# Norm factors folded into output weights, the residual factor folded into norm constants, and pauses in the background weight splitting of a two-layer decoder kernel

## The chip, the core and the metric

The kernel runs on one core of one Trainium2 chip. A core has a matrix engine (TensorE, PE in the profile, with its weight load shown apart as PEld), a vector engine (VectorE, DVE), a scalar engine (ScalarE, ACT), a general engine (GpSimd, POOL), and a queue processor (SyncE, SP) that here issues all transfers between the chip's memory (HBM) and the on-chip buffers (SBUF; matmul results land in PSUM). Each engine works through its own instructions in order and waits on semaphores for the others. The metric is the device time of one execution in microseconds.

## What is computed

Two layers of a decoder trunk over 1024 tokens with 1024 features, in float32. Layer 0 is gated linear attention, layer 1 an indexed sparse attention. The change touches layer 0 only. Cut to what matters:

```python
def gla_mixer(x, ...):                  # layer 0, four heads, 512 value features each
    ...                                 # q, k, v, z, gate from x @ w_in; chunked recurrence gives o
    o = o * rsqrt(mean(o * o, -1) + 1e-5)          # per token and head
    o = o.reshape(B, L, 2048) * gn_g               # one factor per feature
    return (o * silu(z)) @ w_out

for i in range(2):
    y = mixer_i(x)
    x = layer_norm(ALPHA * x + y, ln_g[i], ln_b[i])     # ALPHA = 4 ** 0.25, eps 1e-5
    x = x + (p[i] @ ple_w[i]) * sigmoid(x @ ple_gate_w[i])
```

## The kernel before

**Matmuls in two parts.** Every float32 operand of a large matmul is split in a rounded high part and a low part (high = copy rounded by ACT, low = difference by DVE), and each product is three matmuls: high x high, high x low, low x high. `split` (L387) does so for activations: ACT first, DVE 0.9 us of planned time later.

**Order by a planner.** The program is written out by Python code that keeps a planned time `fl.now`, which grows with each matmul that is issued (`Flow`, L48). Work can be put on a heap with a due time (`at`, `after`, `chain`), and between groups of three matmuls `pace` (L108) issues what is due and then calls the pacers: the weights, and three background generators `bg`, `bg2`, `bg3`. All this decides only the order of instructions on each engine; on the chip the engines keep to that order and wait for semaphores.

**Weights.** `Weights` (L138) loads the 128x1024 weight tiles in the order of `seq` into `wst` (two buffers, L189), and splits each in four steps of 512 columns: two ACT copies into `whi` (L173), two DVE subtractions into `wlo` (L175), one step each 1.15 us of planned time, two to three tiles ahead of their use.

**Splitting ahead.** `split_ahead` (L193) runs in `bg3` during layer 0. Layer 1's weights, used by both halves of the tokens, are split once and the parts stored in HBM. It works in pieces of 512 columns: load `pst` (L200, two buffers), ACT copy `phi` (L209), store `whs` (L211) and load of the next piece, DVE subtraction (L213), store `wls` (L215). A piece takes three turns of the generator; a turn comes when `Background.pace` (L238) finds `now >= due`, and sets `due` on by the gap (2.15). There are 130 pieces.

**Layer 0.** The tokens go in two halves of 512. For each half, `start_half` (L1121) loads x transposed into the tile `y` (L1130) and splits it into the x tiles. Head 0 then runs `v_phase`, `z_phase`, `qk_phase`; after that `load_y` (L1182) loads x again, by tokens, into the same tile `y` (2 MB in one transfer, L1183), where the residual accumulates, and POOL multiplies it by ALPHA (L1185). For each head there follows a stretch in which the recurrence's steps (`core_steps`, L601: s1 to s4 for four chunks of 128 tokens) are spread between the bulk matmuls of the last head's output projection (`out_phase`, L759) and the next head's z (`z_phase`, L587). Names used below: `tr` scores and transposed keys, `kh`, `kl` key parts (L653, L385), `U` the state update, `ot` (L700) the copy of the attention output `o`, `oT` its transpose, `uf` the product with z (L725), `Ah` (L659) the masked scores, `S` (L620, L624) the scaled state.

In `z_phase`, ACT applies SiLU to z and POOL multiplies z by the norm's feature factors `gn` (L593). In s4, POOL makes the per-token factor rs = (ss/512 + eps)^-0.5 (L722, L723), and the output projection's eviction adds psum x rs to y (L752). After the last head `norm_steps` (L781) normalises y; the tail applies the layer norm's gain and the gated embedding.

`g_load` (L457) loads the 16x256 second gate weights of a head three times into `wa2f` (three small transfers, L459), and `g_split` (L461) splits them 8 us of planned time later (ACT L464, then DVE).

Near the end of the first half, small projections of layer 1 are computed (`small_head`, `small_kv`), with its index scores (`index_steps`, L989: matmul `ix`, ACT `rl` L1014, DVE `sc` L1010) between them, while x of the second half is loaded (first piece, a weight tile, second piece, a weight tile, the rest, L1132 to L1138).

Of the kernel before, what the change touches and what calls it, by code (L numbers as in the profile page):

```python
# [10 lines left out]
F32 = mybir.dt.float32  # L11
# [5 lines left out]
AF = mybir.ActivationFunctionType  # L17
# [30 lines left out]
class Flow:  # L48


    def __init__(self, nc):
        self.pe = nc.tensor
        self.now, self.n, self.heap, self.pacers = 0.0, 0, [], []
# [18 lines left out]
    def chain(self, *steps):  # L72

        (_, first), rest = steps[0], steps[1:]
        first()
        if rest:
            self.after(rest[0][0], lambda: self.chain((0, rest[0][1]), *rest[1:]))
# [60 lines left out]
class Weights:  # L138

    def __init__(self, nc, pool, seq, dram, after):
        self.nc, self.pool, self.seq, self.dram, self.after = nc, pool, seq, dram, after
        self.nd = self.ns = self.nu = self.part = 0
        self.due = 0.0
        self.staged, self.parts, self.ahead = {}, {}, {}

    def pace(self, now):
        if now >= self.due and self.step():
# [2 lines left out]
    def step(self):  # L152
        n, i = self.ns, self.part
        if n == len(self.seq):
            return False
        whole = n not in self.staged and self.seq[n][0] in self.ahead
        if n >= self.nu + (3 if whole and self.seq[self.nu - 1][0][0] != "do" else 2):
            return False
        if i == 0:
            if not whole:  # L160
                self.loads(n + 1)
            self.parts[n] = tuple(self.pool.tile([128, 1024], F32R, tag=t, name=t, bufs=4) for t in ("whi", "wlo"))
        if whole:
            for part, there in zip(self.parts[n], self.ahead[self.seq[n][0]]):
                self.nc.sync.dma_start(part.bitcast(F32), there)
            self.ns += 1
            self.loads(min(self.ns + 1, self.nu + 3))
            return True
        st = self.staged[n]
        hi, lo = self.parts[n]  # L170
        c = slice((i % 2) * 512, (i % 2) * 512 + 512)
        if i < 2:
            self.nc.scalar.activation(hi[:, c], st[:, c], AF.Copy)  # L173
        else:
            self.nc.vector.tensor_sub(lo[:, c], st[:, c], hi[:, c].bitcast(F32))  # L175
        self.part = (i + 1) % 4
        if i == 3:
            self.staged.pop(n)
            self.ns += 1
            self.after(1.5, lambda: self.loads(self.ns + 2))  # L180
        return True
# [73 lines left out]
def trunk_kernel(ctx, tc, x_tok, x_T, p_T, pos, freq, g_q, g_k, g_v, g_z, g_a, g_a2, g_ba, g_gn, g_o,  # L255
# [98 lines left out]
    kflip = cp.tile([128, 8], F32, name="kflip")  # L354
    pool.iota(kflip, pattern=[[128, 8]], base=-254, channel_multiplier=1, allow_small_or_imprecise_dtypes=True)
    ba = cp.tile([128, 8], F32, name="ba")
    gn = cp.tile([128, 16], F32, name="gn")
    lngb = cp.tile([128, 2, 2, 8], F32, name="lngb")
    fq = cp.tile([128, 4], F32, name="fq")
    Afs = []  # L360
# [96 lines left out]
    def g_load(h):  # L457
        for i in range(3):
            nc.sync.dma_start(wa2f[32 * i:32 * i + 16, :], g_a2[:, h * 256:(h + 1) * 256])  # L459
# [127 lines left out]
    def z_phase(u, X):  # L587
        h = u["h"]
        zt = lp.tile([128, 4, HT], F32, tag="z", name="z", bufs=2)
        for b in range(4):  # L590
            def ev(ps, b=b):
                def scale():
                    pool.tensor_scalar(zt[:, b], zt[:, b], gn[:, 4 * h + b:4 * h + b + 1], 0.0,  # L593
                                       op0=OP.mult, op1=OP.add)
                    if b == 3:
                        u["z"] = zt
                chain((0, lambda: act.activation(zt[:, b], ps, AF.Silu)), (0.8, scale))

            yield from fm_block(("z", 4 * h + b), X, ev)

    def core_steps(u):  # L601
# [107 lines left out]
        def s4(c):  # L709
            def f():  # L710
                cs = slice(c * 128, c * 128 + 128)
                fl.req(("o", c) in st, "z" in u, h == 0 or u["prev"].get("out", 0) > c)
                ot = st.pop(("o", c))
                ps = pp.tile([128, 4, 128], F32, tag="oT", name="oT")
                for b in range(4):
                    fl.transpose(ps[:, b], ot[:, b * 128:b * 128 + 128], ident)
                uf = lp.tile([128, 4, 128], F32, tag="uf", name="uf", bufs=2)
                uh, ul = t2k("u", F32R), t2k("u", F32R)

                def done():  # L720
                    rc = slice(c, c + 1)
                    pool.tensor_scalar(u["rs"][:, rc], u["ss"][:, rc], 1.0 / 512.0, EPS, op0=OP.mult, op1=OP.add)  # L722
                    pool.tensor_tensor(u["rs"][:, rc], u["rs"][:, rc], mhalf[:, rc], op=OP.pow)  # L723
                    u["u"][c] = uh, ul
                chain((0, lambda: dve.tensor_mul(uf, ps, u["z"][:, :, cs])),  # L725
                      (0.8, lambda: split(uh, ul, uf.rearrange("p b t -> p (b t)"), done)))
            return f
# [50 lines left out]
            P.append((ph, pl))  # L778
        return P

    def norm_steps(y, np_):  # L781

        st8 = np_.tile([128, 4, 2, 6], F32, tag="bn", name="bn")
        mv = np_.tile([128, 4, 2], F32, tag="mv", name="mv")
        rstd = np_.tile([128, 4], F32, tag="rstd", name="rstd")
        f_done = [False] * 4

        def norm(t):
            def power():
                pool.tensor_scalar(rstd[:, t:t + 1], mv[:, t, 1:2], EPS, 1.0, op0=OP.add, op1=OP.mult)  # L790
                pool.tensor_tensor(rstd[:, t:t + 1], rstd[:, t:t + 1], mhalf[:, :1], op=OP.pow)

            def stats():
                for c in range(2):
                    dve.bn_stats(st8[:, t, c], y[:, t, c * 512:c * 512 + 512])  # L795
                dve.bn_aggr(mv[:, t], st8[:, t])
                power()

            def apply():
                dve.tensor_scalar(y[:, t], y[:, t], mv[:, t, 0:1], rstd[:, t:t + 1],  # L800
                                  op0=OP.subtract, op1=OP.mult)
                f_done[t] = True
            chain((0, stats), (2.0, apply))
        return norm, f_done
# [365 lines left out]
    for half in range(NH):  # L1170
# [9 lines left out]
        y = X.y  # L1180

        def load_y(y=y, half=half):  # L1182
            nc.sync.dma_start(y, x_tok[half * HT:(half + 1) * HT, :].rearrange("(t p) d -> p t d", p=128))  # L1183
            for t in range(4):
                pool.tensor_scalar(y[:, t], y[:, t], ALPHA, 0.0, op0=OP.mult, op1=OP.add)  # L1185

        if half == 0:
            for T in range(2):
# [1 line left out]
        for h, u in enumerate(units):  # L1190
            if h == 0:
                fl.run(v_phase(u, X))
                for _ in feeder:
                    pass
                ready = a_phase(X, u.pop("wah"))
                if half == 0:
                    bg.set(rope_tables(), 1.7)

                def first_z():
                    zp = z_phase(u, X)  # L1200
                    for i, _ in enumerate(zp):
                        if i == 6:
                            fl.need(lambda: ready)
                            g_phase(u, ready[0])
                        yield
                fl.run(first_z(), qk_phase(u, X))
                load_y()
                if half == 0:
                    bg.finish()
                    bg3.set(W.split_ahead(later, lp), 2.15)  # L1210
            else:
                fl.need(lambda: "w2" in u)
                g_phase(u, ready[0])
                fl.run(v_phase(u, X), qk_phase(u, X))
            bulk, n = [], 0
            if h:
                bulk.append(out_phase(units[h - 1], y))
                n += 4
            if h < GH - 1:
                g_load(h + 1)  # L1220
                after(8.0, lambda u=units[h + 1]: g_split(u))
                bulk.append(z_phase(units[h + 1], X))
                n += 4
            u["prev"] = units[h - 1]
            steps = core_steps(u)
            spread(steps, fl.now, n * B + 15.5)
            fl.run(*bulk)
            if h == GH - 1:
                Pt = load_p(0, half, lambda: t2k("ah", F32R, 4))
            else:  # L1230
                fl.need(lambda: u.get("late"))
        norm, y_done = norm_steps(y, lp)
        fl.run(out_phase(units[-1], y, norm))
        if half:
            bg.finish()
# [17 lines left out]
        if half == 0:  # L1253
# [15 lines left out]
            rt = lambda: lp.tile([128, HT], F32, tag="ot", name="rl", bufs=2)  # L1269
            steps = [f for T in (2, 3) for f in index_steps(T, scs[T - 2], res, kih, kil, ipsum, rt)]  # L1270
            spread(steps, fl.now + 1.5, 2 * B + 4.5)
            nxt = start_half(1)
            next(nxt[2])

# [323 lines left out]
    for half in range(NH):  # L1598
# [11 lines left out]
        for h, units in enumerate(plan, -1):  # L1610
# [35 lines left out]
            elif h == 4:  # L1646
                bg2.finish()
            fl.run(*(unit(u) for u in units))
        norm, y_done = norm_steps(y, l1)
        if half == 0:  # L1650
            X = XT()
            feed_by(feed_x2(X, 1), fl.now + 5.0, 3.0)
# [78 lines left out]
```

## Time and profile before

| | us |
|---|---|
| median of three runs | 2044.94 (2041.94 to 2046.78) |
| the profiled execution | 2044.36 |
| its span, first to last instruction | 2042.6 |
| PE idle within the span | 70.7 |
| mean granted TensorE clock | 0.992 |

Lines of the profile read thus. A busy line gives for each engine its busy time, its share of the span and its count of instructions. A row of the timeline gives start, length, engine (a q behind it means its sequencer, as in SPq, which issues transfers), line of the code, operation, written tile `<-` read tiles, shape, count, and in square brackets the idle time of that engine just before and what ended it. A row of groups gives count, busy time, mean duration in ns, and idle time before with what ended most of it. `whi<-wst` is the tile whi written from wst; buffer numbers are left out.

### The profile page before, as it was taken

To read this page: it belongs to the slowest core of one execution; us is meant where nothing else is said; L and a number is where in the kernel's file an instruction comes from. 1 tells how busy PE (TensorE), PEld (TensorE's weight loads), DVE (VectorE), ACT (ScalarE), POOL (GpSimd) and SP (SyncE) were. 2 spreads that over 40 slices of the span, in tenths; PEclk is the share of its full clock that TensorE was granted. 3 is DMA by queue.
4 is the path that set the end of the run, shared out by engine and by line. 5 is a ranking of instruction groups with operands and counts; after the bars stand their busy time and mean duration, and the time that the engine had idled before them with its cause. 6 is when DMAs were issued, how large, how long until landed. Compare 5 with 4: busy or idle time off the path is not lost.

```text
span 2042.6 us, 26801 instructions
## 1 busy us (share of the span) xinstructions
PE 1971.9 (97%) x9016; PEld 1616.1 (79%) x9016; DVE 1489.5 (73%) x3037; ACT 1040.1 (51%) x1943; POOL 88.5 (4%) x151
## 2 busy tenths in 40 slices
PE   8899999999899999999999999999999999999999
PEld 6678888887777788888788777888778887878877
DVE  5676666686777787877857978677696887777873
ACT  5564645445465646464445656666432554434432
POOL 0110101010001101010100000000000000000000
PEclk9999999999999999999999999999999999999999
DMA  4457574757856465656557487878856988888774
GB/s 147 172 155 223 167 224 164 223 171 257 286 187 224 146 218 169 223 168 217 179 192 271 152 278 256 302 257 283 276 190 227 333 314 292 299 294 302 256 266 145
DMA packets 173946, 464.96 MB, mean 228 GB/s; under 512 B 20080, under 2 KB 20848, under 8 KB 167664
## 3 DMA queue, kind: packets, MB, share of 16 engines
q1 hardware_dynamic: 173808, 463.25, 67.9%
q8 instruction: 71, 1.16, 0.2%
q14 instruction: 67, 0.55, 0.1%
HBM read 331.18 MB, written 131.99 MB: 227 GB/s over the span
## 4 chain that ended last, share of the span: by engine, by line
PE 75%; DVE 11%; DMA 6%; ACT 5%; issue 2%; SPq 1%; POOLq 0%; ACTq 0%; POOL 0%; DVEq 0%
PE pb L58 55%; PE o L58 7%; PE U L58 6%; PE S L58 5%; DVE wlo L175 1%; DMA wls<-pst 1%; DVE bn L795 1%; DVE sq L1423 1%; DMA sqd<-sq 1%; DMA whi<-whs 1%; DMA xst<-x2s 1%; DMA PT<-sqd 1%; ACT tk L1076 1%; DMA y<-in_x_T 1%; PE oT L62 1%
## 5 line engine op out<-in xcount | busy, mean ns | idle before, releaser
L58 PE MATMUL pb<-x,whi 128*128 128x512 f32 x2272 | 712.5, 395 | 3.7 <-ACT whi L173 2.3
L58 PEld LDWEIGHTS pb<-x,whi 128*128 128x128 f32 x2272 | 418.1, 189 | 84.4 <-ACT whi L173 3.2
L58 PE MATMUL pb<-x,wlo 128*128 128x512 f32 x1136 | 445.1, 392 | 0.5 <-DVE wlo L175 0.5
L58 PE MATMUL pb<-whi,u 128*128 128x512 f32 x1024 | 345.9, 397 | 5.7 <-ACT u L393 4.2
L58 PEld LDWEIGHTS pb<-x,wlo 128*128 128x128 f32 x1136 | 214.3, 189 | 48.7 <-DVE wlo L175 2.7
L175 DVE TENSOR_TENSOR wlo<-wst,whi 128x512 fp32r<-128x512 f32 x296 | 198.2, 686 | 63.1 <-ACT whi L173 62.7
L58 PEld LDWEIGHTS pb<-whi,u 128*128 128x128 f32 x1024 | 193.6, 189 | 47.8 <-ACT u L393 4.8
L173 ACT ACTIVATE whi<-wst 128x512 fp32r<-128x512 f32 x296 | 174.9, 622 | 78.9 <-DMA wst<-in_g_o 19.8
L58 PE MATMUL pb<-wlo,u 128*128 128x512 f32 x512 | 201.6, 394 | 0.0
L209 ACT ACTIVATE phi<-pst 128x512 fp32r<-128x512 f32 x130 | 81.5, 627 | 138.5 <-DMA pst<-in_d_z 34.1
L1417 ACT ACTIVATE sq<-P,mx 128x128 f32<-128x128 f32 (+7 forms) x128 | 99.0, 773 | 86.6 <-DVE mx L1410 60.1
L58 PE MATMUL S<-kT,q 128*128 128x512 f32 (+2 forms) x576 | 122.5, 344 | 0.6 <-DVE q L385 0.6
L1463 ACT ACTIVATE ph<-PT 128x512 fp32r<-128x512 f32 (+1 forms) x160 | 92.7, 601 | 53.5 <-PE o L58 38.4
L1461 DVE TENSOR_TENSOR PT<-PT,ph 128x512 fp32r<-128x512 f32 (+1 forms) x160 | 101.8, 648 | 21.9 <-ACT ph L1463 21.9
L58 PEld LDWEIGHTS S<-kT,q 128*128 128x128 f32 x576 | 100.2, 189 | 19.4 <-DVE mx L1410 1.7
L58 PEld LDWEIGHTS pb<-wlo,u 128*128 128x128 f32 x512 | 97.1, 190 | 18.4
L1076 ACT ACTIVATE tk<-sc,tki 128x768 f16<-128x768 f32 (+2 forms) x90 | 92.8, 1032 | 27.1 <-DVE tki L1085 20.9
L58 PE MATMUL o<-ph,vT 128*128 128x512 f32 (+2 forms) x384 | 101.6, 349 | 4.0 <-ACT ph L1463 4.0
L213 DVE TENSOR_TENSOR pst<-pst,phi 128x512 fp32r<-128x512 f32 x130 | 89.7, 690 | 20.3 <-ACT phi L209 20.2
L1423 DVE STREAM_TRANSPOSE sq<-sq 128x128 f32<-128x128 f32 (+7 forms) x128 | 97.8, 769 | 6.6 <-ACT sq L1417 6.4
L58 PE MATMUL pb<-whi,x 128*128 128x512 f32 x256 | 90.0, 410 | 10.5 <-ACT whi L173 6.1
L1410 DVE CUSTOM_DVE_ANT_0 P<-S,bias 128x512 f32<-128x512 f32 (+3 forms) x128 | 71.2, 561 | 21.1 <-PE S L58 16.7
(311 smaller groups left out, 3282.4 us busy)
## 6 DMA issues: line engine op xcount, KB each, us to landing
whi<-whs SPq DMA_DIRECT2D x130, 512.0 KB
wlo<-wls SPq DMA_DIRECT2D x130, 512.0 KB
sqd<-sq SPq DMA_DIRECT2D x192, 256.0 KB
PT<-sqd SPq DMA_DIRECT2D x48, 1024.0 KB
whs<-phi SPq DMA_DIRECT2D x130, 256.0 KB
wls<-pst SPq DMA_DIRECT2D x130, 256.0 KB
wst<-in_g_v SPq DMA_DIRECT2D x32, 512.0 KB
wst<-in_g_z SPq DMA_DIRECT2D x32, 512.0 KB
```

The source lines that it names most:

```text
L58: self.pe.matmul(out, lhsT, rhs, start=start, stop=stop)
L62: self.pe.transpose(out, in_, ident)
L173: self.nc.scalar.activation(hi[:, c], st[:, c], AF.Copy)
L175: self.nc.vector.tensor_sub(lo[:, c], st[:, c], hi[:, c].bitcast(F32))
L209: self.nc.scalar.activation(hi, st.bitcast(F32), AF.Copy)
L213: self.nc.vector.tensor_sub(st, st.bitcast(F32), hi.bitcast(F32))
L1076: act.activation(junk()[:, :n], scs[j], AF.Sign, bias=cand[:, j:j + 1].bitcast(F32), accum_out=cnt[:, j:j + 1])
L1410: dve.tensor_tensor_reduce(P[:, a:a + e], ps[:, :e], bias_t[T][:, a:a + e], op0=OP.add, op1=OP.min, scale=-ATTN_SCALE, scalar=lim, accum_o ...
L1417: act.activation(to, rows, AF.Exp, scale=-1.0, bias=mx, accum_out=sm[:, t:t + 1])
L1423: dve.transpose(x, x)
L1461: dve.tensor_sub(lo, lo.bitcast(F32), hi.bitcast(F32))
L1463: chain((0, lambda: act.activation(hi, lo.bitcast(F32), AF.Copy)), (0.8, second))
```

## The change

It has three parts.

1. **Factors.** The feature factors `gn` no longer multiply z; they multiply the rows of layer 0's output weights when these are split (the ACT copy takes them as scale, the DVE subtraction becomes a multiply-and-subtract). y is no longer multiplied by ALPHA: y holds x plus mixer / ALPHA, where rs is divided by ALPHA by way of its constants, and the layer norm's eps is divided by ALPHA squared, so that the norm's output is the same.
2. **Order.** The gate weights of head 1 are loaded (`g_load(1)`) ahead of y instead of behind it.
3. **Pauses.** `bg3.due` is set at least 9 us of planned time on at each load of y, and 14 us on where x of the second half is loaded. The gap between its turns goes from 2.15 to 2.1.

```diff
@@ Weights.step
+        key = self.seq[n][0]
+        gain = None
+        if key[0] == "o":
+            row = 4 * key[1] + 2 * key[3] + i % 2
+            gain = self.gains[:, row:row + 1]
         if i < 2:
-            self.nc.scalar.activation(hi[:, c], st[:, c], AF.Copy)
+            self.nc.scalar.activation(hi[:, c], st[:, c], AF.Copy, scale=1.0 if gain is None else gain)
+        elif gain is None:
+            self.nc.vector.tensor_sub(lo[:, c], st[:, c], hi[:, c].bitcast(F32))
         else:
-            self.nc.vector.tensor_sub(lo[:, c], st[:, c], hi[:, c].bitcast(F32))
+            self.nc.vector.scalar_tensor_tensor(lo[:, c], st[:, c], gain, hi[:, c].bitcast(F32),
+                                                op0=OP.mult, op1=OP.subtract)
@@ trunk_kernel
-    gn = cp.tile([128, 16], F32, name="gn")
+    gn = W.gains = cp.tile([128, 16], F32, name="gn")
@@ z_phase
             def ev(ps, b=b):
-                def scale():
-                    pool.tensor_scalar(zt[:, b], zt[:, b], gn[:, 4 * h + b:4 * h + b + 1], 0.0,
-                                       op0=OP.mult, op1=OP.add)
-                    if b == 3:
-                        u["z"] = zt
-                chain((0, lambda: act.activation(zt[:, b], ps, AF.Silu)), (0.8, scale))
+                act.activation(zt[:, b], ps, AF.Silu)
+                if b == 3:
+                    u["z"] = zt
@@ core_steps, s4
-                    pool.tensor_scalar(u["rs"][:, rc], u["ss"][:, rc], 1.0 / 512.0, EPS, op0=OP.mult, op1=OP.add)
+                    pool.tensor_scalar(u["rs"][:, rc], u["ss"][:, rc], ALPHA ** 2 / 512.0, ALPHA ** 2 * EPS,
+                                       op0=OP.mult, op1=OP.add)
@@ norm_steps: eps is now an argument
-                pool.tensor_scalar(rstd[:, t:t + 1], mv[:, t, 1:2], EPS, 1.0, op0=OP.add, op1=OP.mult)
+                pool.tensor_scalar(rstd[:, t:t + 1], mv[:, t, 1:2], eps, 1.0, op0=OP.add, op1=OP.mult)
@@ layer 0
         def load_y(y=y, half=half):
             nc.sync.dma_start(y, x_tok[half * HT:(half + 1) * HT, :].rearrange("(t p) d -> p t d", p=128))
-            for t in range(4):
-                pool.tensor_scalar(y[:, t], y[:, t], ALPHA, 0.0, op0=OP.mult, op1=OP.add)
+            bg3.due = max(bg3.due, fl.now + 9.0)
...
                 fl.run(first_z(), qk_phase(u, X))
+                g_load(1)
                 load_y()
                 if half == 0:
                     bg.finish()
-                    bg3.set(W.split_ahead(later, lp), 2.15)
+                    bg3.set(W.split_ahead(later, lp), 2.1)
...
             if h < GH - 1:
-                g_load(h + 1)
+                if h:
+                    g_load(h + 1)
                 after(8.0, lambda u=units[h + 1]: g_split(u))
...
-        norm, y_done = norm_steps(y, lp)
+        norm, y_done = norm_steps(y, lp, EPS / ALPHA ** 2)
...
             spread(steps, fl.now + 1.5, 2 * B + 4.5)
+            bg3.due = max(bg3.due, fl.now + 14.0)
             nxt = start_half(1)
...
-        norm, y_done = norm_steps(y, l1)
+        norm, y_done = norm_steps(y, l1, EPS)
```

More of the change, by code (lines that the diff above doesn't have):

```diff
@@ L146, in __init__ @@
         self.staged, self.parts, self.ahead = {}, {}, {}
+        self.gains = None
     def pace(self, now):
@@ L779, in load_p, with norm_steps @@
         return P
-    def norm_steps(y, np_):
+    def norm_steps(y, np_, eps):
         st8 = np_.tile([128, 4, 2, 6], F32, tag="bn", name="bn")
```

## The prediction

> **What bounds the kernel now.** I began with the page, whose first parts say how much of the span TensorE (PE) leaves free, then the chain that ended last.
>
> ```profile
> span 2042.6 us, 26801 instructions
> PE 1971.9 (97%) x9016; PEld 1616.1 (79%) x9016; DVE 1489.5 (73%) x3037; ACT 1040.1 (51%) x1943; POOL 88.5 (4%) x151
> PE 75%; DVE 11%; DMA 6%; ACT 5%; issue 2%; SPq 1%; POOLq 0%; ACTq 0%; POOL 0%; DVEq 0%
> ```
>
> PE is busy for 1971.9 of 2042.6 us. The change removes no matmul, so all it can win is a part of the 70.7 us in which PE stands idle, and of the time in which PE runs at a lowered clock. So I looked in the table of stretches for where both occur near the places that the change touches: the two loads of y (88 and 648 us) and the load of x for the second half (541 us).
>
> ```profile
> 90.00:100.00 10.00, 8.59 (x40) 6.47 (x38) 3.03 (x6) 1.62 (x4) 1.16 (x2) 1.00 0.98 355
> 100.00:110.00 10.00, 6.90 (x25) 5.60 (x26) 6.00 (x11) 5.98 (x13) 4.79 (x6) 0.83 0.39 121
> 540.00:550.00 10.00, 5.47 (x27) 4.41 (x25) 5.80 (x11) 4.00 (x8) 0.00 (x0) 1.00 0.83 261
> 550.00:560.00 10.00, 9.24 (x34) 7.36 (x35) 9.08 (x17) 6.30 (x14) 0.00 (x0) 0.83 0.82 310
> 560.00:570.00 10.00, 6.18 (x24) 4.02 (x23) 9.86 (x18) 8.18 (x17) 0.00 (x0) 0.86 0.49 144
> 570.00:580.00 10.00, 10.00 (x37) 7.99 (x37) 9.62 (x26) 5.55 (x12) 0.00 (x0) 0.80 0.73 253
> 660.00:670.00 10.00, 8.33 (x33) 6.66 (x34) 8.92 (x16) 3.50 (x8) 5.75 (x7) 0.83 0.43 135
> ```
>
> Columns: stretch, length, busy time of PE, weight load, VectorE (DVE), ScalarE (ACT), GpSimd (POOL), granted clock, DMA share, GB/s. A clock of 0.83 over 10 us costs (1 - 0.83) x 10 = 1.7 us of matmul work on top of the idle time.
>
> Next the timeline around the first y load shows who holds whom.
>
> ```profile
> 88.44 0.43 SPq L1183 DMA_DIRECT2D y<-in_x_tok  x1
> 90.95 0.42 SPq L200 DMA_DIRECT2D pst<-in_d_ki  x1
> 93.76 0.35 SPq L189 DMA_DIRECT2D wst<-in_g_v  x1
> 100.50 0.63 ACT L209 ACTIVATE phi<-pst 128x512 fp32r<-128x512 f32 x1 [7.70 <-DMA pst<-in_d_ki]
> 101.16 1.28 DVE L213 TENSOR_TENSOR pst<-pst,phi 128x512 fp32r<-128x512 f32 x1 [6.02 <-ACT phi L209]
> 103.10 1.11 PE L62 MATMUL oT<-ident,ot 128*128 128x128 f32 x4 [3.86 <-DVE ot L700]
> ```
>
> y is 2 MB. The first piece of splitting ahead (pst, 256 KB) is issued 2.5 us behind it and lands only at 100.5. ACT, which works in order, stands 7.70 us in front of phi; DVE stands 6.02 us in front of the matching subtraction L213; the copy ot L700, which PE needs for its transposes, is queued behind that subtraction. PE idles 3.86 us and then meets the clock of 0.83.
>
> **The change part by part.**
>
> *Pause at the first y load, and the small load moved ahead of it.* `bg3.due` is set 9 us of planned time on. Two more turns pass before the first phi, so it comes 9 + 2 x 2.1 = 13.2 planned us after the y load instead of about 2. y is gone by then, and pst has 4.2 us to land. What was stuck goes through: 3.86 us of idle time and 1.7 us of clock, **5.6 us**. What is late next is the split of wst g_v, issued at 93.76, also behind y. At the 355 GB/s of the first stretch its 512 KB take 1.5 us and land about 101.5; I come back to it among the rivals. The three small loads of g_load(1) now stand ahead of y on SP and delay its issue by some 2 us (now they fill the 2.5 us from its issue to that of pst). The first reader of y comes far later:
>
> ```profile
> L752 DVE SCALAR_TENSOR_TENSOR y<-pb,rs,y x64: 740/746/752, 182.1 to 1012.8; 128x512 f32<-128x512 f32 x64
> L215 SPq DMA_DIRECT2D wls<-pst x130: 319/327/760, 102.5 to 1032.8; - x130
> 1070.87 0.60 ACT L852 ACTIVATE sg<-pb 128x512 f32<-128x512 f32 x1 [2.73 <-PE pb L58]
> ```
>
> From 90 us to 182.1 there is room for any such delay. The other two rows are for the end of splitting ahead: its last store is at 1032.8, and layer 0 ends behind the sigmoid at 1070.87. The pauses add at most 9 + 9 + 14 = 32 us; 130 pieces of three turns, each 0.05 us closer, give back 19.5. So it ends about 12.5 us later, near 1045, with some 25 us to spare. I cost that at nothing.
>
> *The second y load.* Here bg3 was already running, and the wait comes from two things.
>
> ```profile
> 647.60 0.43 SPq L1183 DMA_DIRECT2D y<-in_x_tok  x1
> 648.08 1.51 SPq L459 DMA_DIRECT2D wa2f<-in_g_a  x3
> 659.61 0.42 ACT L464 ACTIVATE w<-wa2f 128x256 fp32r<-128x256 f32 x1 [3.23 <-DMA wa2f<-in_g_a]
> 660.05 0.57 DVE L385 TENSOR_TENSOR w<-wa2f,w 64x256 fp32r<-64x256 f32 x1 [4.77 <-ACT w L464]
> 661.67 0.50 PE L58 MATMUL U<-v,kl 128*128 128x512 f32 x1 [2.35 <-DVE kl L385]
> ```
>
> wa2f, a few KB, lands behind 2 MB of y, 11.5 us after its issue. ACT waits 3.23 us for it, DVE 4.77 us behind ACT, and kl, for which PE waits, stands behind that on DVE. With g_load(1) ahead of y this goes: 2.35 us of idle time, and the 0.83 of 660 to 670 us, another 1.7: **4.1 us**. The clock is the doubtful half. [...]
>
> *The pause at the x load.* It lasts 14 planned us. Two waits are here, and only one is bg3's.
>
> ```profile
> 541.68 0.50 SPq L189 DMA_DIRECT2D wst<-in_g_v  x1
> 547.87 0.63 ACT L173 ACTIVATE whi<-wst 128x512 fp32r<-128x512 f32 x1 [4.67 <-DMA wst<-in_g_v]
> 549.96 0.88 PE L58 MATMUL ix<-v,u 128*128 128x384 f32 x2 [4.53 <-ACT rl L1014]
> 568.83 1.12 PE L62 MATMUL U<-ident,zz 128*128 128x128 f32 x4 [2.81 <-ACT zz L976]
> L213 DVE TENSOR_TENSOR pst<-pst,phi 128x512 fp32r<-128x512 f32 x3 | 2.1, 684 | 0.0
> ```
>
> (The last row is the grouped view of 545 to 575 us.) The 4.53 us of PE come from whi waiting 4.67 us for its weights, which stand behind what was sent before the pause begins; I leave them (bounds: nothing, and all of it with the 1.7 of the next stretch, 6.2). From 550 to 570 DVE is busy for 9.08 and 9.86 us of 10: there the index scores run on DVE and PE waits for them. The pause takes three subtractions, 2.1 us, out of that, and I count them in full, because DVE has next to no slack there: 2.1 us off gaps that end in the 2.81 (bounds 0 and 2.8). The stretches to 580 hold 1.7 + 1.4 + 2.0 = 5.1 us of lowered clock; a shorter gap may spare one dip of 1.7, and I take half, 0.9. Together **3.0 us**, bounds 0 and 6.2 + 2.8 + 3.4 = 12.4.
>
> *The factors.* Scaling moves into the splits of the 32 output-weight tiles (16 in each half, four pieces each).
>
> ```profile
> L173 ACT ACTIVATE whi<-wst 128x512 fp32r<-128x512 f32 x296 | 174.9, 622 | 78.9 <-DMA wst<-in_g_o 19.8 <-PE pb L58 13.9 <-DMA wst<-in_g_q 13.7
> L620 ACT ACTIVATE S<-R,mid 128x512 fp32r<-128x512 f32 x56 | 39.2, 714 | 0.0
> L175 DVE TENSOR_TENSOR wlo<-wst,whi 128x512 fp32r<-128x512 f32 x296 | 198.2, 686 | 63.1 <-ACT whi L173 62.7
> L624 DVE SCALAR_TENSOR_TENSOR S<-R,mid,S 128x512 fp32r<-128x512 f32 x56 | 42.3, 760 | 1.7 <-ACT S L620 1.5
> L593 POOL TENSOR_SCALAR z<-z,gn 128x512 f32<-128x512 f32 x32 | 24.2, 756 | 392.8 <-ACT z L597 392.8
> L1185 POOL TENSOR_SCALAR y<-y 128x1024 f32<-128x1024 f32 x8 | 9.2, 1173 | 58.6 <-DMA wst<-in_g_v 29.8 <-DMA wa2f<-in_g_a 28.7
> L58 PE MATMUL pb<-whi,u 128*128 128x512 f32 x1024 | 345.9, 397 | 5.7 <-ACT u L393 4.2 <-DVE y L754 1.4
> ```
>
> A copy on ACT whose factor is a column (L620) takes 714 ns against 622: 64 x 92 ns = 5.9 us more ACT. A DVE operation with a column (L624) takes 760 against 686: 64 x 74 = 4.7 us more DVE. POOL loses 24.2 + 9.2 us, and no row of the list of waits names L593 or L1185 as the one waited for. The output matmuls read these tiles, and their row names u and y as what they wait for, never whi: the splits run two to three tiles ahead. So I cost all of it at **nothing**; if the cover were gone, 10.6 us would come back. A gain is excluded by the same rows. The constants of the norms only change values.
>
> *The new rhythm of splitting ahead.* All its later turns fall elsewhere than before.
>
> ```profile
>   ACT phi L209: 115.2, 56
> 134.67 0.50 PE L58 MATMUL pb<-whi,x 128*128 128x512 f32 x1 [1.12 <-ACT z L597]
> 691.65 0.55 PE L62 MATMUL oT<-ident,ot 128*128 128x128 f32 x3 [3.01 <-DVE ot L700]
> ```
>
> phi waits for its load 56 times, 115.2 us in all (first row, from the loads L200), and apart from the stall at 103 us it shows in PE just twice that I found, 1.12 and 3.01 us. Both may vanish (a gain of 4.1) and as much may arise elsewhere; I take zero, bounds -4.1 and +4.1.
>
> The sum is 5.6 + 4.1 + 3.0 = 12.7 us. The profiled execution took 2044.36 us (its span 2042.6 and 1.8 around it), 0.6 below the median of the runs, 2044.94, from which I subtract: **2032.2 us**. Layer 1 is left as it is.
>
> **The rivals.**
>
> *The wait passes to the weights.* y itself, not splitting ahead, fills the queue, so the split of wst g_v takes phi's place: pst, 2.5 us behind y, waited for all of it, and so may the weights. [...] Against it stands the row of the chain for the next chunk:
>
> ```profile
> 110.22 2.04 PE o L58 x9
> ```
>
> By the estimate above the weights land about 101.5 us. What stands behind their split in ACT's queue (the copy Ah) is first needed by these matmuls, which begin 7.1 us behind the transposes of 103.10, so at 106.4 if those start at 99.2 without their idle time. That leaves some 4 us of cover. If it holds all the same, both y terms shrink to a clock dip or so, and with the 3.0 the gain is 0 to 4 us: about 2042.
>
> *Only a part comes.* Either y term is lost, or the x load gives nothing: 12.7 less 3.0 to 8.6, so 4 to 9 us, 2036 to 2041.
>
> *The x load opens up fully.* If traffic of bg3 is what delays the first wst (261 and 310 GB/s in those stretches speak for it, that most was issued before the pause against it), another 6.2 us go: 12.7 + 6.2 = 18.9, 2026.
>
> *The new rhythm costs.* The closer turns (2.1 for 2.15) make phi ask for its load sooner, and phi stalls ACT in heads 1 to 3 of either half just ahead of an eviction or of the copies for the next chunk. One such stall costs PE the mean of the three seen, (3.86 + 1.12 + 3.01) / 3 = 2.7 us, and a dip of 1.7: 4.4. From four more than now on the kernel is slower by over 0.2% (4 x 4.4 = 17.6 against 12.7 + 4.1); with five it is 2032.2 + 22 = 2054. Only 3 of 56 waits show in PE now, so four more are unlikely.
>
> *That it doesn't do what it says* is excluded for the norm, whose output is the same with all of y divided by alpha and eps by its square, and for the pauses as far as bg3 alone reads `due`.
>
> **How the numbers follow.** About 0.2%, 4.1 us, is what a measurement here can tell from no change. Forecast (2029 to 2036) 0.55; opening up fully 0.12; only a part 0.15; the wait passes on 0.12; the rhythm costs 0.06. Faster is 0.55 + 0.12 + 0.15 = 0.82, same 0.12, slower 0.06. The range runs from 2026, the full opening, to 2041, the end of the partial gain; it leaves out the last two cases.
>
> **What would show it.** In the changed profile no phi and no pst load stands within some 9 us behind either y load, the clock stays at 1.00 around 100 and 660 us, and the transposes behind the first y load idle under 1 us. wa2f lands before y, and w (L464) waits for nothing. Between 550 and 570 us PE idles about 2 us less, and the wait of whi for wst g_v near 548 us is still there. The whi splits of the output weights take near 714 ns, their wlo near 760, and PE waits for neither. The last store of splitting ahead falls near 1045 us. I am wrong if whi waits behind y in PE's chain, if dips of the clock appear at new places in heads 1 to 3, or if layer 1, from 1075 us to the end, changes its length.

## The result and the profile after

The changed kernel takes 2030.39 us (median of 4 runs, 2028.46 to 2032.32) against 2045.86 us for the kernel before in the same comparison: a ratio of 0.9927, with a 95% interval of 0.991 to 0.9945. That is 15.5 us by the medians (14.9 by the ratio); 2032.2 was forecast, in a range of 2026 to 2041. The profiled execution has a span of 2026.7 us, 15.9 less than before.

First the page of the changed kernel:

```profile
span 2026.7 us, 26721 instructions
PE 1965.0 (97%) x9016; PEld 1613.9 (80%) x9016; DVE 1488.4 (73%) x3037; ACT 1045.9 (52%) x1943; POOL 53.2 (3%) x111
```

PE stands idle for 2026.7 - 1965.0 = 61.7 us instead of 70.7, so 9.0 of the 15.9 us are idle time. The other 6.9 us are PE's own busy time, with the same 9016 matmuls: it ran less at a lowered clock (mean granted clock 0.996 against 0.992). Then the stretches (columns as in the prediction):

```profile
100.00:110.00 10.00, 10.00 (x51) 8.35 (x51) 8.14 (x15) 4.62 (x11) 0.74 (x2) 1.00 0.43 131
540.00:550.00 10.00, 7.61 (x29) 6.39 (x29) 6.33 (x12) 4.75 (x10) 0.00 (x0) 0.83 0.99 339
550.00:560.00 10.00, 8.67 (x34) 5.71 (x33) 9.83 (x19) 7.54 (x15) 0.00 (x0) 1.00 0.16 38
640.00:650.00 10.00, 9.85 (x41) 8.29 (x42) 6.55 (x16) 2.91 (x7) 0.00 (x0) 0.83 0.88 299
660.00:670.00 10.00, 10.00 (x50) 8.32 (x49) 9.26 (x23) 5.14 (x12) 0.74 (x2) 1.00 0.47 157
```

Behind the first y load PE is now busy for 10.00 of 10 us at full clock (6.90 at 0.83 before). At the second y load the stall at 660 us is gone, but just ahead of the load, at 640 to 650 us, there is a new dip of the clock. The timeline around the first y load shows the new order:

```profile
88.89 1.35 SPq L469 DMA_DIRECT2D wa2f<-in_g_a  x3
90.28 0.42 SPq L1192 DMA_DIRECT2D y<-in_x_tok  x1
94.18 0.35 SPq L199 DMA_DIRECT2D wst<-in_g_v  x1
94.57 0.43 SPq L210 DMA_DIRECT2D pst<-in_d_ki  x1
99.29 0.62 ACT L180 ACTIVATE whi<-wst 128x512 fp32r<-128x512 f32 x1
102.78 0.61 ACT L219 ACTIVATE phi<-pst 128x512 fp32r<-128x512 f32 x1
```

Neither phi nor the weights' split (whi, in ACT's queue ahead of it) waits for anything; no idle time stands in brackets. Note that pst is issued 4.3 us behind y and not 9: the pause is in planned time, which sets a place in a queue, and SP had nothing to wait for when it came to that place. It still had 8.2 us to land, because phi's place in ACT's queue moved too.

The idle times of PE that are left near the three places, and a new one at 411 us:

```profile
412.99 0.50 PE L58 MATMUL o<-v,Al 128*128 128x512 f32 x1 [2.05 <-DVE Al L395]
544.66 1.01 PE L58 MATMUL ix<-v,u 128*128 128x384 f32 x2 [2.39 <-ACT rl L1022]
562.40 1.12 PE L62 MATMUL U<-ident,zz 128*128 128x128 f32 x4 [2.80 <-ACT zz L984]
640.15 0.73 PE L58 MATMUL tr<-ta,m 128*128 128x128 f32 x2 [3.71 <-DVE m L589]
```

PE's sequence of instructions is the same in all kernels here, so the time can be compared stage by stage between the same matmuls in the traces. The marks are: the gate matmul of head 1 (132.9 us before), the first transposes of y in the tail (457.5), the gate matmul of head 0 of the second half (602.4), that of its head 1 (692.8), the first scores of layer 1 (1128.7), the end of the last matmul (2037.6). Changes against before in us, one profiled execution each:

| kernel | start and first y load | heads 1 to 3, first half | x load | second y load | rest of layer 0 | layer 1 |
|---|---|---|---|---|---|---|
| changed | -5.4 | +2.0 | -4.7 | -5.0 | -0.1 | -2.8 |
| factors only | -0.2 | +0.1 | -1.8 | -0.7 | +0.4 | +2.5 |
| order only | +0.8 | +0.2 | -2.0 | +0.3 | +0.3 | +0.8 |
| y pauses and order | -5.8 | +2.3 | -6.2 | -4.6 | +0.5 | +1.4 |
| x pause only | +1.5 | +0.1 | -2.3 | -5.2 | -1.7 | +1.0 |
| changed, no factors | -5.0 | +1.9 | -3.4 | -3.5 | +0.5 | +0.2 |
| changed, no x pause | -7.3 | +2.9 | -1.5 | -6.8 | -0.7 | -1.6 |
| changed, gap 2.15 | -5.8 | +1.7 | -5.7 | -7.3 | +0.3 | -3.1 |
| changed, x pause earlier | -4.1 | +2.1 | -6.5 | -6.7 | +2.7 | -0.9 |
| changed, second y pause earlier | -5.4 | +2.9 | -4.4 | -8.9 | +1.9 | -1.4 |
| changed, first pause 11 | -6.7 | +0.4 | -7.3 | -4.9 | +4.7 | +2.0 |
| both earlier | -4.3 | +2.1 | -6.7 | -5.3 | +3.1 | -0.7 |
| both earlier, first pause 11 | -7.0 | +0.2 | -7.5 | -9.9 | +0.8 | -0.7 |

One execution is not exact. Five of these kernels (changed, no x pause, x pause earlier, second y pause earlier, both earlier) have the same order of instructions up to the x load, and yet their first column runs from -4.1 to -7.3 and their second from +2.0 to +2.9. So a difference of 1 or 2 us in one stage need not be the effect of an edit; a dip of the clock more or less, 10 us at 0.83 as in the rows above, makes 1.7.

Most of the first column's spread is start-up: the matmul at 88.69 us before, just ahead of the first y load, comes at 87.29 to 90.17 us in these kernels. Counted from it to the gate matmul of head 1, the stage takes 38.3 to 38.8 us in the ten kernels that have the first y pause, and 42.9 to 46.2 in the four that lack it (before, factors only, order only, x pause only).

### The profile page after: what moved, and what is told of

Same layout as the page of the kernel before. It is cut to its first block, busy times and chain, and to the rows that moved or that the text cites. A ratio compares the mean times of both kernels' runs of the same rounds, so it can differ in the third digit from the quotient of the medians.

```text
span 2026.7 us, 26721 instructions
## 1 busy us (share of the span) xinstructions
PE 1965.0 (97%) x9016; PEld 1613.9 (80%) x9016; DVE 1488.4 (73%) x3037; ACT 1045.9 (52%) x1943; POOL 53.2 (3%) x111
## 4 chain that ended last, share of the span: by engine, by line
PE 74%; DVE 10%; ACT 6%; DMA 6%; issue 2%; SPq 1%; POOL 0%; POOLq 0%; ACTq 0%; DVEq 0%
PE pb L58 54%; PE o L58 7%; PE U L58 5%; PE S L58 5%; DMA sqd<-sq 1%; DVE sq L1434 1%; DMA pst<-in_d_o 1%; DMA wls<-pst 1%; DVE bn L803 1%; DVE wlo L182 1%; DMA PT<-sqd 1%; ACT whi L180 1%; PE oT L62 1%; DMA xst<-x2s 1%; PE tr L58 1%
## 5 line engine op out<-in xcount | busy, mean ns | idle before, releaser
L182 DVE TENSOR_TENSOR wlo<-wst,whi 128x512 fp32r<-128x512 f32 x232 | 155.1, 685 | 57.9 <-ACT whi L180 57.7
L180 ACT ACTIVATE whi<-wst 128x512 fp32r<-128x512 f32 x232 | 136.4, 622 | 46.6 <-DMA wst<-in_g_z 13.0
L709 ACT ACTIVATE junk<-o 128x512 bf16<-128x512 f32 x32 | 19.1, 597 | 141.0 <-DVE ot L707 136.5
```

What stands on the lines that cost most here:

```text
L180: self.nc.scalar.activation(hi[:, c], st[:, c], AF.Copy, scale=1.0 if gain is None else gain)
```

## The experiments

My theory was that the gain is splitting ahead kept out of the big loads. The rivals were POOL's work, the dearer splits, and a mere shift of the rhythm in which pieces fall.

**One part alone.** The first kernel has part 1 of the change and nothing of parts 2 and 3; against the changed kernel:

```diff
-            bg3.due = max(bg3.due, fl.now + 9.0)
...
-                g_load(1)
                 load_y()
...
-                    bg3.set(W.split_ahead(later, lp), 2.1)
+                    bg3.set(W.split_ahead(later, lp), 2.15)
...
-            if h < GH - 1:
-                if h:
-                    g_load(h + 1)
+            if h < GH - 1:
+                g_load(h + 1)
...
-            bg3.due = max(bg3.due, fl.now + 14.0)
```

> Before, with the factors folded (no POOL work on z and y), but no pauses, the old order and gap. Theory A (the gain is splitting ahead kept out of the loads): within 2 us of before, ACT and DVE each some 5 us busier in layer 0, the idle times of 3.86 us at 103, 2.35 us at 661 and the clock dips behind them still there. Theory B (much of the gain is POOL's 33 us gone, which had slowed DVE or held y): faster by 4 us or more. Theory C (uncovered cost of the dearer splits): slower by 3 to 10 us, with PE waiting for whi or wlo of the output weights.

2044.8 us against 2044.49, ratio 0.9999 (0.9988 to 1.001): nothing that can be measured, neither POOL's absence nor the dearer splits. Its row at the first y load, from the timeline:

```profile
101.56 0.69 DVE L223 TENSOR_TENSOR pst<-pst,phi 128x512 fp32r<-128x512 f32 x1 [5.57 <-ACT phi L219]
102.91 0.66 PE L62 MATMUL oT<-ident,ot 128*128 128x128 f32 x4 [2.79 <-DVE ot L707]
```

The stall is there (2.79 us, a little less than 3.86). Some 0.6 us of the difference are the subtraction ahead of ot, which takes 0.69 us here; before it took 1.28, at a time when POOL was multiplying y:

```profile
98.84 4.51 POOL L1185 TENSOR_SCALAR y<-y 128x1024 f32<-128x1024 f32 x4 [28.74 <-DMA wa2f<-in_g_a]
```

ACT is 5.3 us busier in all (1045.4 against 1040.1), as expected, but DVE is not (1488.9 against 1489.5): other rows of it got shorter by about as much as the splits got longer. What the splits cost shows in the groups of the changed kernel:

```profile
L180 ACT ACTIVATE whi<-wst,gn 128x512 fp32r<-128x512 f32 x64 | 44.1, 713 | 14.2 <-DMA wst<-in_g_o 12.2 <-PE pb L58 1.8
L184 DVE SCALAR_TENSOR_TENSOR wlo<-wst,gn,whi 128x512 fp32r<-128x512 f32 x64 | 47.0, 747 | 4.9 <-ACT whi L180 4.8
```

713 and 747 ns, against 714 and 760 taken from neighbours: 64 x (713 - 622) = 5.8 us of ACT and 64 x (747 - 685) = 4.0 us of DVE, hidden.

The second kernel has part 2 and the y pauses of part 3:

```diff
             nc.sync.dma_start(y, x_tok[...])
+            bg3.due = max(bg3.due, fl.now + 9.0)
...
+                g_load(1)
                 load_y()
...
-                g_load(h + 1)
+                if h:
+                    g_load(h + 1)
```

> Before, with the two pauses at the y loads and the gate weights of head 1 ahead of y; no factors, no pause at the x load, gap 2.15. Theory A: faster by some 9.7 us (5.6 at the first y load, 4.1 at the second), idle time at both places under 1 us. Rival (the wait passes to the weights): faster by under 4 us, with whi waiting for wst behind y and PE behind it.

2033.3 us, ratio 0.9943 (0.9929 to 0.9958), by the ratio 11.7 us faster. Of these, -5.8 and -4.6 us, 10.4 together, are in the two stages where they were expected. But heads 1 to 3 lose 2.3 and the x load, which this kernel doesn't touch, wins 6.2.

The third has only the pause at the x load:

```diff
+            bg3.due = max(bg3.due, fl.now + 14.0)
             nxt = start_half(1)
```

> Before, with the pause of 14 us at the x load alone. Theory A: faster by some 3 us; the wait of whi for the first wst near 548 us remains, DVE has 2 us less between 550 and 570 us. Rival (bg3's traffic delays that wst): that wait falls from 4.7 to under 2 us, faster by 6 us or more. Rival (only a new rhythm for all later pieces): no more than 1 us better at 550 to 575 us and other idle times behind it.

2037.31 us, ratio 0.9958 (0.9942 to 0.9974). In its own stage it wins 2.3 us, and whi there still waits (5.42 us). The larger part, 5.2 us, comes at the second y load, where it changes nothing but the moment at which pieces fall. So the gains of single parts do not add: by the ratios the two kernels' 11.7 and 8.6 us make 20, while the whole change has 14.9 and the next kernel, which joins just these two and the gap of 2.1, has 11.0.

The fourth leaves only the factors out of the change; against the changed kernel, in short (the subtraction and the constants of the norms go back too):

```diff
-            self.nc.scalar.activation(hi[:, c], st[:, c], AF.Copy, scale=1.0 if gain is None else gain)
+            self.nc.scalar.activation(hi[:, c], st[:, c], AF.Copy)
...
+                    pool.tensor_scalar(zt[:, b], zt[:, b], gn[:, 4 * h + b:4 * h + b + 1], 0.0,
+                                       op0=OP.mult, op1=OP.add)
...
+            for t in range(4):
+                pool.tensor_scalar(y[:, t], y[:, t], ALPHA, 0.0, op0=OP.mult, op1=OP.add)
```

> The changed kernel without its first part: order, all three pauses and gap 2.1, but z and y scaled by POOL as before. Theory A: as fast as the changed kernel, within 2 us. Theory B (POOL's work matters): 4 us or more slower than the changed kernel. If the idle time of 2.05 us at 411 us (PE for Al, behind dearer subtractions on DVE) is owed to the factors, it is gone here and this kernel is some 2 us faster there.

2034.51 us, ratio 0.9946 (0.993 to 0.9961) against the changed kernel's 0.9927: the intervals overlap, and no difference between the two is settled. The new idle time at 411 us is there too (1.91 us), so the factors are not its cause.

**The order alone.** I had put the second y stall down to wa2f behind y, and had argued that from the trace only. Against the kernel before:

```diff
+                g_load(1)
                 load_y()
...
-                g_load(h + 1)
+                if h:
+                    g_load(h + 1)
```

> Before, with the gate weights of head 1 loaded ahead of y as the only edit. My split of the second y term: the wait of ACT for wa2f (3.2 us) and the idle time of 2.35 us at 661 us go even without a pause, if that wait is the cause; then a piece's phi near 660 us is the next wait and a part of the gap returns: 1 to 3 us faster between 645 and 693 us. At the first y load nothing changes (idle 3.9 us and the dip remain). In all 0 to 4 us faster.

2044.47 us, ratio 1.0 (0.9992 to 1.0009). The wait for wa2f is gone and nothing is won, where I had expected 1 to 3 us. The timeline of this kernel shows why:

```profile
647.78 0.42 SPq L1183 DMA_DIRECT2D y<-in_x_tok  x1
658.78 0.33 SPq L200 DMA_DIRECT2D pst<-in_d_z  x1
662.27 0.63 ACT L209 ACTIVATE phi<-pst 128x512 fp32r<-128x512 f32 x1 [5.20 <-DMA pst<-in_d_z]
663.63 0.50 PE L58 MATMUL o<-v,Ah 128*128 128x512 f32 x1 [1.66 <-ACT Ah L659]
```

phi now waits 5.20 us in wa2f's place, and Ah, for which PE waits, is queued behind phi on ACT. Removing the last wait in a queue uncovered the next. With the y pauses on top (the second kernel above) PE waits neither for kl nor for Ah there. No kernel has the pause without the new order, so what the order adds to it is open; and the kernel with the x pause alone won 5.2 us in this stage with neither of the two, so a shift of the rhythm can do as much.

**What the x pause gives, and what it misses.** Against the changed kernel:

```diff
-            bg3.due = max(bg3.due, fl.now + 14.0)
             nxt = start_half(1)
```

> The changed kernel without the pause at the x load. The prediction's term: 3.0 us slower than the changed kernel, DVE 2 us busier between 545 and 570 us. Rival (in the sum the x pause gives nothing, since the kernel with the y pauses alone was as fast in layer 0 as the whole change): within 1.5 us, with other idle times in place of the ones saved.

2033.33 us, ratio 0.9943 (0.9925 to 0.9961); the interval overlaps the changed kernel's, so in all no difference is settled. Without the pause the x stage is 4.7 - 1.5 = 3.2 us slower than in the changed kernel, and 1.8 us of it come back at the second y load. About half of the 3.2 is clock (granted 0.80 in 545 to 570 us, against 0.87 in the changed kernel, or some 1.7 us). The 2 us more of DVE do not show: it is busy for 23.91 us of those 25, against 23.80. And the kernel with the y pauses and the order, which has no x pause either, stands at -6.2 in this stage, so the rhythm moves it as much as the pause does. The next kernel begins the pause one and a half blocks earlier:

```diff
+                for i, _ in enumerate(small_head(0, ...)):
+                    if i == 27:
+                        bg3.due = max(bg3.due, fl.now + 14.0)
```

> The changed kernel, with a first pause of splitting ahead already over the last one and a half blocks before the x load (14 us from the 28th turn of the small head), the 14 us at the x load kept. If bg3's traffic delays the first weight tile of the second half: the wait of whi there falls from 4.5 to under 2.5 us, PE's gap of 2.4 us in front of ix goes, 2 to 4 us faster than the changed kernel up to the end of the index scores. My theory (that wait is x's and the weights' own traffic): the wait stays at 4 us or more, and the time within 2 us of the changed kernel apart from what a new rhythm does behind.

My theory fell here. From the timelines, first the changed kernel, then this one:

```profile
531.32 0.41 SPq L225 DMA_DIRECT2D wls<-pst  x1
534.72 0.63 ACT L219 ACTIVATE phi<-pst 128x512 fp32r<-128x512 f32 x1 [1.04 <-DMA pst<-in_d_q]
535.38 0.32 SPq L221 DMA_DIRECT2D whs<-phi  x1
536.72 0.42 SPq L199 DMA_DIRECT2D wst<-in_g_v  x1
543.08 1.15 ACT L180 ACTIVATE whi<-wst 128x512 fp32r<-128x512 f32 x2 [4.46 <-DMA wst<-in_g_v]
```

```profile
529.81 0.86 SPq L199 DMA_DIRECT2D wst<-in_g_v  x1
539.84 1.15 ACT L180 ACTIVATE whi<-wst 128x512 fp32r<-128x512 f32 x2
```

Without the last pieces ahead of it the weight tile is issued 6.9 us earlier, and whi waits for nothing. SP works in order: in the changed kernel it issues nothing from 531.73 to 535.38, until phi is made, which whs stores, and x and the weights stand behind that store. The longer first pause (below) shows the same by its rhythm alone: there the tile is issued at 532.00, and whi waits 0.65 us. The 2.39 us in front of ix are gone (a later ix has 0.68), and the stage goes from -4.7 to -6.5. In all it is not faster (2030.88 us, 0.9933, 0.9917 to 0.9948): the rest of layer 0 gives back 2.8.

**The second y load.** The 3.71 us at 640 us are owed to a piece just ahead of the pause. From the changed kernel's timeline:

```profile
638.14 0.63 ACT L219 ACTIVATE phi<-pst 128x512 fp32r<-128x512 f32 x1 [3.38 <-DMA pst<-in_d_o]
638.80 0.69 DVE L223 TENSOR_TENSOR pst<-pst,phi 128x512 fp32r<-128x512 f32 x1 [1.89 <-ACT phi L219]
639.41 0.68 DVE L589 TENSOR_TENSOR m<-pb,m 128x512 f32<-128x512 f32 x1
```

m, for which PE waits, is queued behind that piece's subtraction. So the pause was begun earlier:

```diff
+                        if half and i == 20:
+                            bg3.due = max(bg3.due, fl.now + 10.0)
```

> The changed kernel, with the pause of the second half beginning already in the second k block but one piece earlier (10 us from the 21st turn of q and k), the pause at the load itself kept. Theory: the new idle time of 3.71 us at 636 us (PE for m, behind a piece's subtraction whose phi waited for its load) and the dip behind it are a piece that falls just ahead of the pause. Then that gap falls to about 1 us, and the kernel is 2.5 to 4.5 us faster than the changed one. Rival (the gap is DVE's own work there): it stays above 2.5 us and nothing is won.

The gap falls to 0.93 us and the stage goes from -5.0 to -8.9, as expected; the sum does not: 2031.35 us, 0.9935 (0.9919 to 0.9951), not faster than the changed kernel. The rest of layer 0 gives back 2.0. The 0.9 us in heads 1 to 3 lie ahead of the edit and cannot be its doing; a dip of the clock stands there in this profile (last section).

**The rhythm.** Two kernels move all later pieces and change nothing else; against the changed kernel they read:

```diff
-                    bg3.set(W.split_ahead(later, lp), 2.1)
+                    bg3.set(W.split_ahead(later, lp), 2.15)
```

```diff
-            bg3.due = max(bg3.due, fl.now + 9.0)
+            bg3.due = max(bg3.due, fl.now + (9.0 if half else 11.0))
```

> The changed kernel with the gap of 2.15 between turns as before. If only the sum of the waits of phi counts: within 1.5 us. If it is the rhythm that sets where pieces fall: layer 0 differs by 2 to 6 us either way, and the idle time of 2.05 us at 411 us (PE for Al) moves or goes; the last store of splitting ahead is some 15 to 20 us later.

> The changed kernel with the first pause 11 us long instead of 9, so that every later piece of the first half falls 2 us later against the heads. If the new idle time of 2.05 us at 411 us comes from a piece that falls just ahead of Al in the DVE queue, it moves or goes (under 1 us there), and 1 to 3 us are won in head 3. Rival (it is the load of that stretch itself): it stays at about 2 us.

The gap of 2.15 gives 2026.8 us, 0.9918 (0.9898 to 0.9938); the x stage and the second y load win 1.0 and 2.3 us over the changed kernel, layer 0 as a whole 3.7, and the stall at 411 us stays (2.12 us). The last store of splitting ahead is at 1056.5 instead of 1034.4. The longer first pause gives 2027.47 us, 0.9922 (0.9908 to 0.9937), and does away with that stall. DVE's timeline in the changed kernel, then in this one:

```profile
409.45 0.69 DVE L223 TENSOR_TENSOR pst<-pst,phi 128x512 fp32r<-128x512 f32 x1 [1.83 <-ACT phi L219]
...
412.65 0.28 DVE L395 TENSOR_TENSOR Al<-Af,Ah 128x128 fp32r<-128x128 f32 x1
```

```profile
409.60 0.28 DVE L395 TENSOR_TENSOR Al<-Af,Ah 128x128 fp32r<-128x128 f32 x1
...
411.72 0.69 DVE L223 TENSOR_TENSOR pst<-pst,phi 128x512 fp32r<-128x512 f32 x1
```

With the piece behind Al instead of ahead of it, Al comes at 409.60 instead of 412.65 (the two profiles are 0.7 us apart at the start of head 3) and PE does not wait: heads 1 to 3 go from +2.0 to +0.4. Behind the second y load this kernel stands at +4.7, though, where the changed one has -0.1. The intervals of both kernels overlap the changed one's: what is shown here are stages and stalls, not a faster kernel.

**Together.** The last two kernels join edits that are shown above: the two earlier pauses, and these with the first pause of 11 us.

> The changed kernel with both earlier pauses, at the x load and at the second y load. If each takes away its own wait, the gains seen alone add up to the end of head 0 of the second half: 1.8 + 3.9 us there over the changed kernel, some 3 to 5 us faster in all (about 2026 us). If a new rhythm gives back elsewhere what is won: within 2 us of the changed kernel.

> The same with the first pause 11 us long. If the three gains add: 1 to 3 us faster than the kernel with both earlier pauses, about 2024 us; if the rhythm decides, within 2 us of it.

Both earlier pauses: 2030.94 us, 0.9938 (0.9925 to 0.995), no gain over the changed kernel. The 3.71 us are gone, but a piece behind the pause now hits (timeline of this kernel):

```profile
671.41 0.63 ACT L219 ACTIVATE phi<-pst 128x512 fp32r<-128x512 f32 x1 [4.23 <-DMA pst<-in_d_q]
676.41 1.11 PE L62 MATMUL oT<-ident,ot 128*128 128x128 f32 x4 [4.42 <-DVE ot L707]
```

With the first pause at 11 us as well: 2023.73 us (5 runs), 0.9895 (0.9879 to 0.9911). Its interval all but parts from the changed kernel's (0.9911 against 0.991) and is clear of those of the kernels with either earlier pause alone (from 0.9917 and 0.9919); it overlaps those of the two kernels of the rhythm. By its median it is the fastest kernel of the study. The time is the one expected, about 2024, but the step is not: it is 7.2 us faster than the kernel with both earlier pauses, where 1 to 3 were to come if the gains add. All three stages keep their gains (-7.0, -7.5, -9.9; the -7.5 of the x stage is about what the longer first pause had alone) and heads 1 to 3 give back nothing. That the rhythm happens to suit it is part of that: the same three pauses with 9 us gained nothing.

## Why the prediction was right

By the ratio's interval the gain is 11.3 to 18.4 us, so the 12.7 forecast and the 15.5 of the medians are not told apart. One of the three terms came as it was worked out; the other two came out near their size through other gaps than those named.

*First y load, 5.6 us forecast.* Right in place, cause and size: the stage shows -5.4 (-5.8 without the start-up), the changed kernel has no idle time and clock 1.00 at 100 to 110 us, and all ten kernels with this pause are alike there. The order alone left the stall as it was (3.90 us), so it is the pause. The rival that the weights take phi's place did not come; whi at 99.29 waits for nothing.

*Second y load, 4.1 us forecast.* The size was right by luck (-5.0), the cause was not. I gave the gain to g_load(1) standing ahead of y; alone that brought +0.3. The 2.35 us did go, and with them most of the stall of 3.01 us at 691 that I had left at zero (0.79 is left); against that the idle time ahead of tr grew from 1.90 to 3.71 us, with a dip of its own. The step that failed is reading the last wait on ACT as the only one.

*x load, 3.0 us forecast.* Taking the pause out costs 3.2 us there, half of it clock, and the pause alone won 2.3; within what single profiles can tell the size fits, and no more can be said, since other rhythms move this stage as much. But the term was worked out from the wrong gap: the 2.81 us ahead of the transposes of zz, from which I took 2.1, are 2.80 after, though DVE was relieved. The saving lies in the gap I had left alone (4.53 to 2.39 us), in the smaller ones and in a dip. Between the first bounds, that gap could give its full 6.2 us; the kernel with the earlier pause shows that bg3 was indeed the main cause, through SP's order, and that the pause begins too late to take it all. The step that failed is taking the relief of DVE for the gain.

*The factors, nothing forecast.* Right: 0.9999 alone (0.9988 to 1.001).

*The new rhythm, zero with bounds of 4.1 either way.* This is the term that counted most and was worked out least. In the changed kernel it cost 2.0 us in heads 1 to 3 and won some at 691 us; over the kernels of this study single stages move by up to 5 us with it, dips of the clock included.

*Layer 1, unchanged.* It was 2.8 us shorter. Its stretches in the two kernels, and in the one with the factors only:

```profile
1128.67:2042.58 913.91, 885.30 (x4127) 729.23 (x4126) 680.19 (x1472) 437.81 (x879) 11.67 (x17) 0.99 0.77 263
```

```profile
1115.60:2026.70 911.10, 882.98 (x4127) 727.59 (x4126) 680.10 (x1472) 437.78 (x879) 11.69 (x17) 1.00 0.77 264
```

```profile
1126.50:2042.90 916.40, 887.25 (x4127) 730.70 (x4126) 680.11 (x1472) 437.58 (x879) 11.71 (x17) 0.99 0.77 262
```

The same 4127 matmuls keep PE busy for 885.30, 882.98 and 887.25 us, while DVE and ACT do the same work in the same time. In stretches of 10 us from its first scores on, the clock dips three times in layer 1 before (stretches of 0.83, 0.66, and 0.85 with 0.98) and twice in the changed kernel (0.83 each): 6.8 and 3.4 us by (1 - clock) x 10. So in these two it is mostly the dips of the clock that differ, and with them the stretch, which changes by -3.1 to +2.5 us over these thirteen profiles with no edit to layer 1. A changed length of layer 1 was one of the signs of being wrong; it came, but nothing here ties it to the change. Of the 15.9 us of the profile 13.1 are layer 0's (12.7 forecast), and draws of the clock are in these too. Splitting ahead ended at 1034.4, not 1045; its cost was nothing, as forecast.

## What to carry to other kernels

Here a background stream that shares in-order engines with the main work cost little by its work and much by where it stood: one piece waiting for its load held all that was queued behind it, on ACT (5.20 us for phi in the kernel with the order alone), on DVE (1.89 us for its subtraction ahead of m in the changed kernel) and also in the issuing queue (3.65 us without an issue on SP from 531.73 us). Keep it out of the stretch around a big transfer, and begin the pause some turns before that transfer, not at it: here this won in its own stage each time, though in the whole only together with a rhythm that suited. Judge such an edit by stage, between the same instructions of two traces, since here each shift of the rhythm moved stalls elsewhere and the gains of single edits did not add. Compare also kernels that are the same up to the edit: what differs there is chance.

## What the hardware showed beside that

Eight of the kernels have an idle time of 1.91 to 2.12 us ahead of the same matmul near 411 us. Behind it the clock dipped in three of them (idle 1.96, 2.05 and 2.06 us) and not in the other five (1.91, 2.05, 2.06, 2.06 and 2.12). The stretch behind it in three, first with the second y pause earlier, then without the x pause, then in the changed kernel:

```profile
411.00:421.00 10.00, 7.99 (x33) 6.66 (x34) 8.39 (x15) 3.42 (x8) 0.74 (x2) 0.83 0.39 119
```

```profile
411.00:421.00 10.00, 9.88 (x41) 8.21 (x42) 8.55 (x16) 3.79 (x9) 0.74 (x2) 0.83 0.39 134
```

```profile
411.00:421.00 10.00, 8.02 (x40) 6.55 (x40) 8.50 (x16) 3.42 (x8) 0.74 (x2) 1.00 0.40 130
```

Idle times of 2.05 and 2.06 us end either way here, and 1.96 us were enough for a dip where 2.12 us had none. So the length of such a stall does not tell in these traces whether a dip comes behind it, and these dips, some 1.7 us each by the 0.83 of 10 us, cannot be forecast one by one.
